# A two-layer mixer and experts kernel: three-part float32r products replaced by plain float32 products, experts' weights loaded in runs of 8 KB into 18 buffers

## The chip, the cores and the metric

The kernel runs on one core of one Trainium2 chip. The metric is the device time of one execution in microseconds (us); lower is better. Six units matter here: TensorE (PE in the profile, with its weight loads as PEld), VectorE (DVE), ScalarE (ACT), GpSimd (POOL), the queue of SyncE (SP) that issues most transfers, and the DMA engines that carry them out.

## What is computed

One sequence of 1024 tokens with 1024 features passes through two layers in float32. Each layer adds a mixer and then a routed block of experts, both on a normed and modulated input:

```
for i in range(2):
    shift1, scale1, gate1, shift2, scale2, gate2 = split(silu(c) @ ada_w[i] + ada_b[i], 6)
    h = modulate(rmsnorm(x, norm_mix_w[i]), shift1, scale1)
    y = even_mixer(h, ...) if i == 0 else odd_mixer(h, ...)
    x = x + gate1 * y
    h = modulate(rmsnorm(x, norm_ffn_w[i]), shift2, scale2)
    x = x + gate2 * hierarchical_moe(h, ...)
return rmsnorm(x, final_norm_w)
```

The even mixer is a product with `w_in` (1024 x 2048), a state space part with a gated product, stick-breaking attention over eight heads, and a product with `w_out`. The odd mixer has the same frame with a recurrence (rwkv7) and a second state space part (mamba2). Each token goes to two of 32 experts. An expert computes `(silu(x w_gate) * (x w_up)) w_down` with 1024 x 512, 1024 x 512 and 512 x 1024 weights: 6.29 MB per expert and layer, each read once from DRAM or, for an expert with more than 128 tokens, once per further block.

## The kernel before

**Products.** TensorE multiplies a stationary tile of 128 x 128 with a moving one of up to 512 columns and adds over blocks of 128 features. The large products are made in float32r, in three parts. `split` (L136) makes of a tile `x` a high part (a copy on ScalarE that rounds to float32r, L138) and a low part (`x` less the high part, on VectorE, L139). `mm3` (L237, products at L240 to L242) adds high x high, high x low and low x high into the same sum. For the experts the local function `three` does the same (L815 to L817), and `halves` (L803) splits a weight tile of 128 x 2048 in two pieces per part into rings of four tiles.

```
138        self.nc.scalar.activation(hi, x, AF.Copy)
139        self.nc.vector.tensor_tensor(lo, x, hi.bitcast(FT), op=OP.subtract)
240        nc.tensor.matmul(p, a[0], b[0], start=first, stop=False)
241        nc.tensor.matmul(p, a[0], b[1], start=False, stop=False)
242        nc.tensor.matmul(p, a[1], b[0], start=False, stop=last)
```

**Where three-part products stand.** Layer 0: the projections (`proj_T` and `proj_v`, 256 products of 512 columns), the gated product of the state space part (`glu`, 64), and the output product of tiles 2 to 7 (`out_rows`, 96; tiles 0 and 1 are made by plain float32 products at L681, ahead of the splitting of the output weights). Layer 1: the projections of the first half of the tokens (`o_group` and `m_dt`, 216), those of the second half (216), and the output product of the last three tiles (48). The projections of the second half run as work in the background: `project` is a generator that yields what each step is taken to cost (0.64 us per product), and `poke` draws 1.2 us worth of steps after each step of the recurrence. All else on TensorE, the transposes (L106) among it, is plain float32 or bfloat16.

**Experts (`moe`).** One block of 128 rows after another: 33 blocks written out per layer and more behind branches that the routing decides (two such blocks ran in layer 0). For a block, POOL gathers the rows (L786), `turn` transposes them (eight transposes into two PSUM tiles), eight products per part make the gate and eight the up product, ScalarE and VectorE make `silu(g) * u` (L831, L832), four transposes turn it, eight products make the two halves of the result, VectorE scales them (L847), and POOL scatters the rows to DRAM (L848). That is 24 products, 72 parts, and 12 transposes per block. PSUM holds one gate, one up, one hidden, two transposed and three result tiles. The products of one block and those of the next lie interleaved; a scheduler puts every engine's instructions in order when the kernel is built.

**Weights on their way.** `ring` opens pools of tiles of 128 x 2048 floats (1 MB); `wtile` takes them in turn. `wload` (L74) issues the load on SP's queue, with feature `k * 128 + p` on partition `p`, so that the runs in DRAM are 2 KB (gate, up) or 4 KB (down). The experts have 10 such buffers: `a0`, `c0`, `b0` with two each and `d0` with four in layer 0, `a1`, `c1`, `b1`, `e1` in layer 1. SP's queue works in order: a load that waits for its buffer holds up all loads behind it.

**Output stage.** `out_norm` (layer 1) and the end of `even` (layer 0) split the four output weight tiles once into `o["wp"]`, make the output product tile by tile, add it to the rows of x (loaded by SP, L1857 in layer 0) and route the tile (`out_route`). The four weight buffers are free as soon as they are split.

## Time and profile before

| | |
|---|---|
| runs shown | 3290.62, 3296.51, 3298.77 us; median 3296.51 us |
| profiled execution, span from first to last instruction | 3303.1 us (its own time is not listed apart) |
| instructions | 42136 |
| PE busy | 2817.3 us, 85% of the span, 15141 matmul records |
| DVE, ACT, POOL busy | 71%, 47%, 28% |
| moved by DMA | 704.06 MB, mean 213 GB/s |

The profile gives for each engine the time in which it worked on an instruction. Matmuls overlap, so a record's duration is longer than the distance to the next one; where the rate matters, the distance of starts is to be read. The granted clock of TensorE is given per stretch as a share of 2.4 GHz; 0.5 is its lower level of 1.2 GHz, and values between are means over both. A line of the code can be that of a helper, so L106 stands for every transpose.

### The profile page before, as it was taken

Reading aid. Unit: us, or ns where it says so; the run is one execution under the profiler, and the core shown is the slowest. Engines: PE = TensorE matmul, PEld = TensorE weight load, DVE = VectorE, ACT = ScalarE, POOL = GpSimd, SP = SyncE. Lnnn points to the kernel's source line nnn. Section 1 sums busy time; section 2 is a strip of 40 time slices with the busy share of each in tenths; the row PEclk is TensorE's granted clock in tenths of the full one; section 3 lists DMA queues with packets and bytes.
Section 4 is the critical chain, followed back from the end, with each engine's and each line's share of the span. In section 5 each row is a group of like instructions: output and inputs, shape, how many; then the busy total and the mean of one; then the engine's idle time right before and its main releaser. Section 6 shows DMA issues by size and latency. Waiting matters only on the chain. (4 is left out here: it accounts for less than half of the span.)

```text
span 3303.1 us, 42136 instructions
## 1 busy us (share of the span) xinstructions
PE 2817.3 (85%) x15141; PEld 2220.7 (67%) x15141; DVE 2350.0 (71%) x3738; ACT 1566.8 (47%) x2280; POOL 912.7 (28%) x1177
## 2 busy tenths in 40 slices
PE   5986788988899998997479999998895999998981
PEld 4775556656677776776367777776785777776761
DVE  7456998557789987886644445645558789987884
ACT  4211456333567766764334323332232667766661
POOL 4342654234221111110300533344125122111111
PEclk9987889988899999998689878887996999999996
DMA  8756201334899998984844522253355799998967
GB/s 274 162 146 162 78 15 46 109 131 145 308 292 380 354 338 293 343 278 160 273 147 129 175 65 86 74 138 101 97 190 206 275 293 373 360 338 302 350 243 297
DMA packets 473363, 704.06 MB, mean 213 GB/s; under 512 B 119681, under 2 KB 261025, under 8 KB 470577
## 3 DMA queue, kind: packets, MB, share of 16 engines
q1 hardware_dynamic: 400928, 642.69, 58.1%
q0 software_dynamic: 19872, 33.60, 2.8%
q10 hardware_dynamic: 52336, 24.87, 2.7%
q8 instruction: 128, 2.10, 0.3%
q14 instruction: 99, 0.80, 0.1%
HBM read 651.69 MB, written 88.16 MB: 224 GB/s over the span
## 5 line engine op out<-in xcount | busy, mean ns | idle before, releaser
L139 DVE TENSOR_TENSOR wlo<-w,whi 128x1024 fp32r<-128x1024 f32 x816 | 956.9, 1217 | 182.2 <-ACT whi L138 180.4
L138 ACT ACTIVATE whi<-w 128x1024 fp32r<-128x1024 f32 x816 | 811.0, 1052 | 415.3 <-PE ps_g L817 244.9
L240 PE MATMUL ps_b<-hTh,wh 128*128 128x512 f32 x608 | 261.8, 432 | 37.8 <-ACT cc L1242 21.2
L848 POOL DMA_INDIRECT ye_d<-y,tab x64 | 132.4, 2069 | 479.5 <-DVE y L847 393.5
L786 POOL DMA_INDIRECT xg<-h_d,tok x64 | 107.0, 1671 | 559.9 <-PE ps_t L106 525.9
L241 PE MATMUL ps_b<-hTl,wh 128*128 128x512 f32 x608 | 257.8, 424 | 0.3 <-DVE hTl L139 0.3
L242 PE MATMUL ps_b<-hTh,wl 128*128 128x512 f32 x608 | 256.2, 421 | 0.0
L816 PE MATMUL ps_g<-wlo,xh 128*128 128x512 f32 x544 | 228.1, 419 | 30.8 <-DVE wlo L139 30.7
L815 PE MATMUL ps_y<-whi,hh 128*128 128x512 f32 x544 | 225.2, 414 | 24.4 <-DVE y L847 11.4
L815 PE MATMUL ps_g<-whi,xh 128*128 128x512 f32 x544 | 224.8, 413 | 20.7 <-ACT xh L138 19.6
L817 PE MATMUL ps_g<-whi,xl 128*128 128x512 f32 x544 | 222.4, 409 | 1.6 <-DVE xl L139 1.4
L816 PE MATMUL ps_y<-wlo,hh 128*128 128x512 f32 x544 | 221.1, 406 | 0.0
L815 PE MATMUL ps_u<-whi,xh 128*128 128x512 f32 x544 | 217.1, 399 | 1.0 <-ACT whi L138 1.0
L816 PE MATMUL ps_u<-wlo,xh 128*128 128x512 f32 x544 | 216.3, 398 | 0.0
L817 PE MATMUL ps_u<-whi,xl 128*128 128x512 f32 x544 | 214.9, 395 | 0.0
L817 PE MATMUL ps_y<-whi,hl 128*128 128x512 f32 x544 | 212.0, 402 | 0.9 <-DVE hl L139 0.9
L139 DVE TENSOR_TENSOR wl<-w,wh 128x1024 fp32r<-128x1024 f32 x84 | 105.5, 1268 | 100.0 <-ACT wh L138 99.2
L240 PEld LDWEIGHTS ps_b<-hTh,wh 128*128 128x128 f32 x608 | 126.1, 208 | 67.4 <-ACT cc L1242 22.8
L167 DVE SCALAR_TENSOR_TENSOR adacc<-w,cs,adacc 128x256 f32<-128x256 f32 x329 | 163.5, 514 | 5.2
L138 ACT ACTIVATE wh<-w 128x1024 fp32r<-128x1024 f32 x84 | 86.3, 1053 | 161.2 <-PE ps_b L241 149.3
L816 PEld LDWEIGHTS ps_g<-wlo,xh 128*128 128x128 f32 x544 | 106.4, 196 | 68.1 <-DVE wlo L139 47.4
L313 DVE TENSOR_TENSOR_SCAN sP<-keep,sP,sbz 128x256 f32<-128x256 f32 (+1 forms) x160 | 131.5, 865 | 23.6 <-POOL keep L307 12.5
(658 smaller groups left out, 6039.9 us busy)
## 6 DMA issues: line engine op xcount, KB each, us to landing
w<-in_moe_w_down_dram SPq DMA_DIRECT2D x138, 1024.0 KB
w<-in_moe_w_up_dram SPq DMA_DIRECT2D x138, 1024.0 KB
w<-in_moe_w_gate_dram SPq DMA_DIRECT2D x138, 1024.0 KB
w<-in_ada_w_dram SPq DMA_DIRECT2D x48, 1024.0 KB
w<-in_odd_w_in_dram SPq DMA_DIRECT2D x26, 1024.0 KB
cy<-ye_d SPq DMA_DIRECT2D x16, 1024.0 KB
cx<-xm_d SPq DMA_DIRECT2D x29, 512.0 KB
w<-in_even_w_in_dram SPq DMA_DIRECT2D x8, 1024.0 KB
```

The lines of the kernel that those rows point to most:

```text
L138: self.nc.scalar.activation(hi, x, AF.Copy)
L139: self.nc.vector.tensor_tensor(lo, x, hi.bitcast(FT), op=OP.subtract)
L167: eng.scalar_tensor_tensor(acc, wk, ck, acc, op0=OP.mult, op1=OP.add)
L240: nc.tensor.matmul(p, a[0], b[0], start=first, stop=False)
L241: nc.tensor.matmul(p, a[0], b[1], start=False, stop=False)
L242: nc.tensor.matmul(p, a[1], b[0], start=False, stop=last)
L313: v.tensor_tensor_scan(P[:, r, 0:n][:, ::-1], keep[:, r, 0:n][:, ::-1], zero.to_broadcast([128, n]), P[:, r, n:n + 1], op0=OP.mult, op1=OP ...
L786: nc.gpsimd.indirect_dma_start(out=xg, out_offset=None, in_=h_d[:], in_offset=bass.IndirectOffsetOnAxis(ap=tokc, axis=0), bounds_check=T - ...
L815: nc.tensor.matmul(p, xh[:, k, :], w[0][:, j, ns], start=first, stop=False)
L816: nc.tensor.matmul(p, xh[:, k, :], w[1][:, j, ns], start=False, stop=False)
L817: nc.tensor.matmul(p, xl[:, k, :], w[0][:, j, ns], start=False, stop=last)
L848: nc.gpsimd.indirect_dma_start(out=ye_d[:], out_offset=bass.IndirectOffsetOnAxis(ap=asgc, axis=0), in_=y, in_offset=None, bounds_check=2 * ...
```

## The change

Every three-part product becomes one plain float32 product; `split`, `wsplit`, `mm3`, `halves` and `three` go, and with them all split tiles. Normed inputs are written once as float32; one saved half of the tokens in layer 1 goes to DRAM as one tensor of 2 MB instead of two. The experts' weights are loaded by `wload_runs` (L73 of the changed kernel): partition `p` takes the features `p * k` to `p * k + k - 1`, a run of 8 KB. So that the features meet, `turn` and the transposes of the hidden values read every fourth and every second column. The rings hold 18 buffers: `d0` has eight and a new ring `f0` four in layer 0, `e1` has 13 in layer 1. The generators of the background work yield 0.43 per product. The output weights are used from the buffers into which they were loaded.

```
+    def wload_runs(self, src, k):
+        w = self.wtile()
+        self.nc.sync.dma_start(w, src.rearrange("(p k) n -> p (k n)", k=k))
+        return w[:].rearrange("p (k n) -> p k n", k=k)
...
     def proj_T
-                self.mm3(p[:, h, :], [x[:, k, col:col + 128] for x in w], [x[:, k, ts] for x in hs], k == 0, k == KD - 1)
+                self.nc.tensor.matmul(p[:, h, :], w[:, k, col:col + 128], hT[:, k, ts], start=(k == 0), stop=(k == KD - 1))
...
     def turn
-                    self.transpose(pt[:, q * 128:(q + 1) * 128], xg[:, (hh * 4 + q) * 128:(hh * 4 + q + 1) * 128])
-                self.split(xh[:, 4 * hh:4 * hh + 4, :].rearrange("p k t -> p (k t)"),
-                           xl[:, 4 * hh:4 * hh + 4, :].rearrange("p k t -> p (k t)"), pt)
+                cols = xg[:, hh * 512:(hh + 1) * 512].rearrange("t (p k) -> t k p", k=4)
...
+                    self.transpose(pt[:, q * 128:(q + 1) * 128], cols[:, q, :])
+                if hh == 0:
+                    nc.scalar.activation(o, pt, AF.Copy)
+                else:
+                    nc.vector.tensor_copy(o, pt)
...
     def expert
-                for h in range(2):
-                    w = halves(ww[h])
-                    for k in range(4):
-                        three(p, x, 4 * h + k, w, k, slice(0, 512), h == 0 and k == 0, h == 1 and k == 3)
+                for k in range(KD):
+                    nc.tensor.matmul(p, x[:, k, :], ww[k // 4][:, k % 4, :], start=(k == 0), stop=(k == KD - 1))
...
+                cols = hs[:, (q // 2) * 256:(q // 2) * 256 + 256].rearrange("t (p k) -> t k p", k=2)
+                self.transpose(pt[:, q * 128:(q + 1) * 128], cols[:, q % 2, :])
...
-            for f2 in range(2):
-                w = halves(ws[2][f2])
-                for f in range(2):
-                    for n in range(2):
-                        three(py[n], h, 2 * f2 + f, w, f, slice(n * 512, (n + 1) * 512), f2 == 0 and f == 0, f2 == 1 and f == 1)
+            for f in range(4):
+                for n in range(2):
+                    nc.tensor.matmul(py[n], h[:, f, :], ws[2][f // 2][:, f % 2, n * 512:(n + 1) * 512],
+                                     start=(f == 0), stop=(f == 3))
...
     def o_group
-            self.mm3(p, [x[:, k, :] for x in w], [x[:, k, :] for x in hs], k == 0, k == KD - 1)
-            yield 0.64
+            self.nc.tensor.matmul(p, w[:, k, :], hs[:, k, :], start=(k == 0), stop=(k == KD - 1))
+            yield 0.43
...
     def even
-            o["wp"] = [self.wsplit(w, wx, 4) for w in o["ws"]]
...
-            keep.enter_context(self.ring("d0", 4))
+            keep.enter_context(self.ring("d0", 8))
             right.close()
+            keep.enter_context(self.ring("f0", 4))
...
-        c1.enter_context(k.ring("e1", 5))
+        c1.enter_context(k.ring("e1", 13))
```

The order of instructions moves at two places. First TensorE in the expert loop of layer 0, once it is even. `ps_g` and `ps_u` are the gate and up sums, `ps_y` the result, `ps_t` transposed rows, `ps_h` transposed hidden values; `whi`, `wlo`, `xh`, `xl` are high and low parts. Before, a piece of one block:

```order
L106 MATMUL ps_h<-ident,hs 128x128 x4
L106 MATMUL ps_t<-ident,xg_6610 128x128 x8
L815 MATMUL ps_u<-whi,xh 128x512
L816 MATMUL ps_g<-wlo,xh 128x512
L817 MATMUL ps_g<-whi,xl 128x512
```

In the changed kernel, one whole block:

```order
L111 MATMUL ps_t<-ident,xg_5571 128x128 x4
L784 MATMUL ps_g<-w,xt 128x512 x4
L111 MATMUL ps_t<-ident,xg_5573 128x128 x4
L111 MATMUL ps_h<-ident,hs 128x128 x4
L784 MATMUL ps_u<-w,xt 128x512 x3
L784 MATMUL ps_g<-w,xt 128x512 x4
L784 MATMUL ps_u<-w,xt 128x512 x3
L798 MATMUL ps_y<-w,hh 128x512 x8
L784 MATMUL ps_u<-w,xt 128x512 x2
```

A block's 72 parts are 24 products, still interleaved with those of the next block, and the result's eight stand together; products of another block stand between the hidden transposes and the result that needs them.

Second, SP's queue from the output stage of layer 0 on. `xo` are the rows of x that the output product is added to. Before:

```order
L1857 DMA xo<-in_x_dram 128x1024 x2
L77 DMA w<-in_moe_w_down_dram 128x2x1024 x2
L77 DMA w<-in_moe_w_up_dram 128x4x512 x2
L77 DMA w<-in_moe_w_gate_dram 128x4x512 x2
L1857 DMA xo<-in_x_dram 128x1024 x6
L77 DMA w<-in_moe_w_gate_dram 128x4x512 x2
```

In the changed kernel:

```order
L1807 DMA xo<-in_x_dram 128x1024 x2
L76 DMA w<-in_moe_w_down_dram 128x2048 x2
L76 DMA w<-in_moe_w_gate_dram 128x2048 x2
L76 DMA w<-in_moe_w_up_dram 128x2048 x2
L76 DMA w<-in_moe_w_down_dram 128x2048 x2
L76 DMA w<-in_moe_w_gate_dram 128x2048 x2
L1807 DMA xo<-in_x_dram 128x1024 x5
L76 DMA w<-in_moe_w_up_dram 128x2048 x2
L76 DMA w<-in_moe_w_gate_dram 128x2048 x2
L1807 DMA xo<-in_x_dram 128x1024
```

More of the experts' weights are asked for ahead of the rows, and the last load of rows, that of tile 7, has moved behind the up and gate loads of the first expert (the four just ahead of it), which take the buffers `c0` and `a0` that hold the output weights.

## Rows read from the trace of the kernel before

**Rows 1.** The page, first lines: the span, and busy time per engine.

```profile
span 3303.1 us, 42136 instructions
PE 2817.3 (85%) x15141; PEld 2220.7 (67%) x15141; DVE 2350.0 (71%) x3738; ACT 1566.8 (47%) x2280; POOL 912.7 (28%) x1177
```

**Rows 2.** The page's groups: count, busy us, mean ns, idle time before.

```profile
L139 DVE TENSOR_TENSOR wlo<-w,whi 128x1024 fp32r<-128x1024 f32 x816 | 956.9, 1217 | 182.2 <-ACT whi L138 180.4
```

**Rows 3.** Timeline of PE in the expert loop: start, us, instruction, idle before.

```profile
1059.74 0.50 PE L816 MATMUL ps_g<-wlo,xh 128*128 128x512 f32 x1 [0.45 <-DVE wlo L139]
1060.07 0.39 PE L817 MATMUL ps_g<-whi,xl 128*128 128x512 f32 x1
...
1062.40 0.39 PE L815 MATMUL ps_g<-whi,xh 128*128 128x512 f32 x1
1062.63 0.60 PE L106 MATMUL ps_h<-ident,hs 128*128 128x128 f32 x4
...
1063.86 0.48 PE L815 MATMUL ps_u<-whi,xh 128*128 128x512 f32 x1
...
1078.55 0.50 PE L816 MATMUL ps_g<-wlo,xh 128*128 128x512 f32 x1 [0.45 <-DVE wlo L139]
```

**Rows 4.** Timeline of weight loads at the plain products of layer 0.

```profile
701.95 0.19 PEld L681 LDWEIGHTS ps_e<-w,gl 128*128 128x128 f32 x1 [0.24 <-issue]
...
707.10 0.19 PEld L681 LDWEIGHTS ps_e<-w,qT 128*128 128x128 f32 x1 [0.24 <-issue]
```

**Rows 5.** Instructions on tile `ps_e`: count, duration min/median/max ns, first and last start.

```profile
L681 PE MATMUL ps_e<-w,gl x32: 592/592/697, 648.3 to 704.5; 128*128 128x512 f32 x32
```

**Rows 6.** Timeline of DVE: first and 33rd block of layer 0, then layer 1.

```profile
853.29 0.68 DVE L832 TENSOR_TENSOR hs<-hs,ps_u 128x512 f32<-128x512 f32 x1
...
1505.79 0.68 DVE L832 TENSOR_TENSOR hs<-hs,ps_u 128x512 f32<-128x512 f32 x1
...
2576.33 0.68 DVE L832 TENSOR_TENSOR hs<-hs,ps_u 128x512 f32<-128x512 f32 x1
...
3229.39 0.69 DVE L832 TENSOR_TENSOR hs<-hs,ps_u 128x512 f32<-128x512 f32 x1 [0.42 <-PE ps_u L817]
```

**Rows 7.** Stretches: us, busy (instructions) per engine, granted clock, DMA share, GB/s.

```profile
1021.00:1136.00 115.00, 112.16 (x516) 89.91 (x516) 106.46 (x111) 85.34 (x100) 22.97 (x14) 1.00 1.01 360
1250.00:1345.00 95.00, 82.24 (x354) 64.62 (x355) 76.24 (x80) 60.44 (x70) 12.57 (x9) 0.96 0.87 300
...
3260.00:3280.00 20.00, 0.00 (x0) 0.00 (x0) 15.09 (x15) 3.45 (x6) 4.49 (x3) 0.50 1.02 425
```

**Rows 8.** Stretches, line L240 alone (first parts): us, PE, PEld, clock, DMA.

```profile
59.00:290.00 231.00, 106.67 (x256) 51.52 (x256) 0.93 0.64 166
555.00:648.00 93.00, 27.09 (x64) 12.54 (x64) 0.93 0.27 80
708.00:799.00 91.00, 38.85 (x96) 18.00 (x96) 1.00 0.43 145
1600.00:1840.00 240.00, 93.72 (x224) 44.09 (x224) 0.87 0.55 184
1840.00:2200.00 360.00, 92.84 (x208) 43.97 (x208) 0.85 0.32 89
2453.00:2506.00 53.00, 20.05 (x48) 9.33 (x48) 0.96 0.56 204
```

**Rows 9.** The background stretch of layer 1, all instructions, columns as in rows 7.

```profile
1840.00:2200.00 360.00, 353.99 (x2640) 273.69 (x2639) 192.35 (x373) 113.52 (x223) 152.13 (x388) 0.85 0.32 89
```

**Rows 10.** Waits of PE in 59 to 290 us: total us, times, longest.

```profile
PE ps_e L179 <- DVE adacc L167: 10.9, 5, 3.4
PE ps_b L240 <- ACT hTh L138: 8.7, 1, 8.7
```

**Rows 11.** Timeline at the start of layer 0's experts: SP's queue, then PE.

```profile
709.98 76.30 SPq L1857 DMA_DIRECT2D xo<-in_x_dram  x6
...
797.79 0.39 PE L242 MATMUL ps_e<-wh,yl 128*128 128x512 f32 x1
...
838.35 1.94 PE L106 MATMUL ps_t<-ident,xg 128*128 128x128 f32 x8 [21.07 <-issue]
```

More of the change, by code (lines that the diff above doesn't have):

```diff
@@ L10 @@
 FT = mybir.dt.float32
-FR = mybir.dt.float32r
 BF = mybir.dt.bfloat16
@@ L755, in out_norm @@
                 else:
-                    yt = self.out_y(o, t, y_d)
-                    y = [oy.tile([128, KD, 128], FR, name=n) for n in ("yh", "yl")]
-                    self.split(*y, yt)
-                    x = self.out_rows(o, t, lambda k: [h[:, k, :] for h in y], "a")
+                    y = self.out_y(o, t, y_d)
+                    x = self.out_rows(o, t, lambda k: y[:, k, :], "a")
                 self.out_route(o, t, x, "bcb")
@@ L1173, in odd_setup @@
         R["cc"] = one.tile([128, 8, 3], FT, name="cc")
-        R["wd"] = [one.tile([128, KD, 8], FR, name=n) for n in ("wdh", "wdl")]
-        self.split(*R["wd"], R["wdt"])
         R["tk"] = one.tile([128, NT, 2, 8], FT, name="tk")
@@ L1211, in m_dt @@
         for k in range(KD):
[L1212 to L1213 removed]
+            nc.tensor.matmul(p[0:8, :], R["wdt"][:, k, :], hs[:, k, :], start=(k == 0), stop=(k == KD - 1))
+            yield 0.43
         nc.scalar.activation(xx, p[0:8, :], AF.Identity, bias=R["dtb"])
@@ L1698, in odd @@
             pj = right.enter_context(tc.tile_pool(name="wsp1", bufs=1, side="right"))
-            hs = [hp.tile([128, KD, 512], FR, name=n) for n in ("hTh", "hTl")]
+            hs = hp.tile([128, KD, 512], FT, name="hT")
             rw = [(128 * c, self.rw_shift, c) for c in (12, 4, 6, 0, 2, 8, 10)]
@@ L1715, in getx @@
                     return x, junk, junk
-                ht = [np_.tile([128, KD, 512], FR, name=n) for n in ("tTh", "tTl")]
+                ht = np_.tile([128, KD, 512], FT, name="tT")
                 for t in range(4):
@@ L1736, in project @@
                     for z in range(2):
-                        w = [pj.tile([128, KD, 128], FR, name=x, bufs=2) for x in ("wh", "wl")]
-                        self.split(*w, src[:, :, 128 * z:128 * z + 128])
-                        yield from do(h, c + z, w, hs, R, pj)
+                        yield from do(h, c + z, src[:, :, 128 * z:128 * z + 128], hs, R, pj)
                     pos[0] = n + 1
@@ L1938, in out @@
                 ts = slice(t * 128, (t + 1) * 128)
-                if t < XA:
-                    return self.out_rows(o, t, lambda k: gl[:, k, ts] if k < 4 else qT[:, k - 4, ts], "e")
-                y = [wx.tile([128, KD, 128], FR, name=n) for n in ("yh", "yl")]
-                for z, src in enumerate((gl, qT)):
-                    self.split(*(x[:, 4 * z:4 * z + 4] for x in y), src[:, :, ts])
-                return self.out_rows(o, t, lambda k: [x[:, k, :] for x in y], "e")
+                return self.out_rows(o, t, lambda k: gl[:, k, ts] if k < 4 else qT[:, k - 4, ts], "e")
             def route(t, x):
@@ L1974, in even @@
             keep.enter_context(self.ring("b0", 2))
-            parts = ExitStack()
-            wx = pool(parts, "wx0", "left")
-            o["wp"] = [self.wsplit(w, wx, 4) for w in o["ws"]]
             for t in range(NT):
```

108 lines of the change are left out of this document (32 added, 76 removed).

## The prediction

> **What bounds the kernel now.** I read the busy shares first: TensorE is busy for 2817 of 3303 us, VectorE for 71% [rows 1]. Shares are averages, so I went to the expert loops, where 33 blocks per layer stand between 853.29 and 1505.79 us and between 2576.33 and 3229.39 us [rows 6]: 32 intervals in 652.5 and 653.1 us, 20.4 us a block. The reader should see that this is not one limit but two that alternate. At its tightest a block takes 18.81 us, and TensorE idles once in it, 0.45 us, for a low part of the weights [rows 3]; over 1021 to 1136 us it is busy 112 of 115 us at full clock. From 1250 to 1345 us four blocks take some 23.5 us each, TensorE is busy 82 of 95 us, and the DMA moves only 300 GB/s at a share of 0.87 [rows 7]: weights come late there, because a load must wait until a buffer has been split. So the loop is TensorE's at best (18.8) and the weights' at worst, 20.4 in the mean.
>
> Outside the loops the three-part products stand in six stretches; their counts of first parts, and so of products, are 256, 64, 96, 224, 208 and 48, together 896 (layer 1's projections are cut at 1840 us) [rows 8]. In the long background stretch of layer 1 TensorE is busy 354 of 360 us at a granted clock of 0.85 of full speed (a mix of 1.2 and 2.4 GHz) [rows 9].
>
> **The price of one product.** Eleven parts start from 1060.07 to 1062.40 us, ten steps of 0.233 us; that makes 0.699 us for a three-part product of 512 columns [rows 3]. The kernel before already holds plain float32 products of the same shape: the first two output tiles of layer 0. They have 32 records for 2 tiles x 2 halves x 4 feature blocks = 16 products [rows 5], two records each. Thirteen weight loads of such records start from 701.95 to 707.10 us, in twelve even steps: 0.429 us a record, **0.858 us a plain product** [rows 4]. The change therefore costs 0.159 us per product wherever TensorE sets the pace. That is the number the forecast rests on; the instruction count falls to a third, the time does not.
>
> **Part 1, the expert blocks.** 24 products: 24 x 0.858 = 20.6 us. Twelve transposes take 1.23 us (1062.63 to 1063.86) [rows 3]. Of the tight block 18.81 - 72 x 0.233 - 1.23 = 0.80 us is left for joints; 0.45 of that is the wait for a split, which goes, 0.4 stays. Sum 22.2. The transposes now read every fourth (rows) or every second (hidden) float, because the weights lie in runs of 8 KB and the features must be dealt out the same way. No row shows such a read; I bound it by nothing below and by twice the transposes' 0.103 us each above, 0 to 1.2 us a block, and take 0.1, near the rows that exist. **22.3 us a block.** The splits (VectorE 957 us over both loops [rows 2], ScalarE nearly as much) were beside TensorE's work, so removing them returns only the 1.6 us by which the mean block exceeds the tight one; that cover is gone as the limit moves to TensorE. Against 20.4: +1.9 x 66 = **+125 us**.
>
> Does the DMA keep up? A block needs 6.29 MB of weights and some 0.5 MB of rows, 6.8 MB in 22.3 us = 305 GB/s. The loop reached 360 GB/s over 1021 to 1136 us; a stretch that reads runs of 8 KB (the expert outputs, at the end) and writes reaches 425 [rows 7]. With 18 buffers, 12 blocks' parts ahead of the 6 in use, a slow stretch is bridged. So the long runs and the buffers are worth nothing beyond the 1.6 us already counted. A buffer is now held until the product has read it, not only until it was split; that is what the eight more buffers pay for.
>
> The Trainium skill, "SBUF — State Buffer" (The DMA port swizzle), speaks against part of this: SBUF has lines of 16 bytes, and a reader needs two hits a line for full speed, which every fourth float does not give. No run here shows it; by that page the row transposes would be slower, and by rival 2 below the sum would be 47 us more.
>
> **Part 2, the start of the loops.** In layer 0 the four buffers that the first expert's gate and up weights take still hold the output weights, which formerly were split away. The order shows these four loads now ahead of the last load of x rows on SP's queue; they wait for the last output product, and the row load behind them waits too. Before, the last x load had been issued 76.30 us after 709.98, so 11.5 us ahead of the last output part at 797.79, and 40.6 us passed from there to the first expert transposes at 838.35 [rows 11]. Four loads of 1.05 MB at 300 to 360 GB/s [rows 7] are 12 to 14 us. Routing of the tile before hides about half: +7 us, ends 0 and +13. In layer 1 two of these loads stood there before: +4, same ends. **+11 us.**
>
> **Part 3, the other products.** At 0.159 us each: 40.7, 10.2, 15.3, 35.6, 33.1 and 7.6, together 142 us. What absorbs some:
> - Layer 0's projections wait 10.9 us for partial sums of the conditioning and 8.7 for a split of the normed rows [rows 10]. A later TensorE hides most of the first, and the modulation without its split shortens the second; VectorE is relieved in the norm as well: -22, leaves +18.
> - The gated product of layer 0: a little split waiting goes, +6. Output tiles: +15, nothing covers them.
> - Layer 1, first half of the tokens: the norm loses two passes per quarter tile on ScalarE and VectorE: -10, +25.
> - The background stretch has 6 us of idle time in 360 [rows 9], so nearly all stays: +28. Its generators count a step as 0.43 instead of 0.64, so three products go between two foreground steps where two went; the same work stands earlier, in total no less. The output tiles after it: +7.
>
> **+99 us**; ends 60 (twice the cover) and 142 (none). VectorE's removed splits in these stages are else beside TensorE, so nothing more comes back.
>
> **Sum.** 125 + 11 + 99 = +235 us on the span of 3303.1, so 3538 us. The page gives this execution's span and no further time of its own; the span is 6.6 us above the median of the runs, 3296.5. Moving the median by the same 235 gives **3531 us**.
>
> **Rivals.**
> 1. **A plain product costs one record, not two.** If its two records overlapped, or a product took one, it would cost 0.43 us, the figure that the pacing of the background work uses. A block would fall to 24 x 0.43 + 1.6 = 11.9 us and the weights would set 6.8 MB / 360 GB/s = 18.8: -1.6 x 66 = -106; the others 896 x 0.27 = -241, of which some 190 count: about 3000 us. It decides at about 0.75 us per product, where 235 us over some 2,280 effective products is gone. Against it stand the counts [rows 5] and the even spacing [rows 4]. Chance 0.03; some idle time of TensorE (486 us in all) shrinking more than I count could bring no change or a small gain, 0.03 more.
> 2. **The strided transposes.** If the eight row transposes take twice their 0.103 us, a block takes 0.8 us instead of 0.1 more: +0.7 x 66 = +47, 3578 us. For it: it is an access no row covers, and all of it is on TensorE's path. The page named in part 1 says that such a read is slow. Against: the weight load of a transpose runs beside the one before. Chance 0.14.
> 3. **The DMA becomes the limit.** If the runs of 8 KB move at 250 GB/s, a block takes 27 us: +4.9 x 66 = 323 more, some 3850 us. For it: the loop was short of weights at 300 GB/s in one stretch. Against: 425 GB/s at a share of 1.02 elsewhere [rows 7]. Chance 0.06.
>
> That the splits might stay in the program is excluded by the order: no such row is left on VectorE.
>
> **Numbers.** The forecast has 0.74, rivals 0.26. Low end: a block at 21.8 (-33), twice the cover in part 3 (-39), no late start (-11): 3448, rounded to 3440. High end: rival 2 (+47), no cover (+43), late starts in full (+15): 3636, rounded to 3640. Beyond lie rivals 1 and 3, together about 0.1, and the sizes I misjudge. A measurement of this kernel tells 0.3%, 10 us, from no change. Faster 0.04 (rival 1 and part of the idle time), same 0.02, slower 0.94.
>
> **What would show it.** In the profile after: two records per product, 0.43 us apart; blocks spaced 22 to 23 us by the product of the hidden values, evenly, without the 24 to 26 us ones; TensorE above 95% in the loops at full clock; VectorE and ScalarE far below; DMA about 300 GB/s and below its full share. Transposes further apart than 0.103 us would mean rival 2, TensorE idle before products and a full DMA share rival 3. A last x load issued only after the last output product would confirm part 2. I am wrong if products start closer than 0.8 us, or if the blocks are not TensorE's.

## The result and the profile after

The changed kernel takes 3513.1 us (median of 4 runs, 3506.1 to 3522.5), the kernel before 3295.0 us (4 runs): a ratio of 1.066, 95% interval 1.064 to 1.069, 218 us slower. The forecast was 3531 us, slower, range 3440 to 3640.

The first lines of the page of the changed kernel answer to [rows 1]. TensorE's share rises from 85 to 90% with fewer records; VectorE's falls from 71 to 35%, ScalarE's from 47 to 18%.

```profile
span 3520.8 us, 34468 instructions
PE 3176.6 (90%) x12613; PEld 1748.9 (50%) x12613; DVE 1225.1 (35%) x2643; ACT 625.4 (18%) x1251; POOL 758.8 (22%) x1177
```

TensorE's timeline in layer 0's expert loop, one block (start, us, instruction), is the counterpart of [rows 3]. There is no idle time in it, and every product shows as two records.

```profile
1094.80 0.63 PE L111 MATMUL ps_t<-ident,xg 128*128 128x128 f32 x4
1095.27 3.60 PE L784 MATMUL ps_g<-w,xt 128*128 128x512 f32 x8
1098.71 0.63 PE L111 MATMUL ps_t<-ident,xg 128*128 128x128 f32 x4
1099.18 0.65 PE L111 MATMUL ps_h<-ident,hs 128*128 128x128 f32 x4
1099.66 2.74 PE L784 MATMUL ps_u<-w,xt 128*128 128x512 f32 x6
1102.24 3.60 PE L784 MATMUL ps_g<-w,xt 128*128 128x512 f32 x8
1105.67 2.74 PE L784 MATMUL ps_u<-w,xt 128*128 128x512 f32 x6
1108.25 7.03 PE L798 MATMUL ps_y<-w,hh 128*128 128x512 f32 x16
1115.11 1.88 PE L784 MATMUL ps_u<-w,xt 128*128 128x512 f32 x4
1116.83 0.63 PE L111 MATMUL ps_t<-ident,xg 128*128 128x128 f32 x4
```

Sixteen records of the result start from 1108.25 to 1115.11 us: 6.86 / 16 = 0.429 us each, 0.858 us a product, the price that the forecast took from [rows 4]. The whole block, from 1094.80 to 1116.83, takes 22.03 us = 24 x 0.858 + 1.44 for the twelve transposes. VectorE's timeline at the product of the hidden values, first and last of the 33 blocks per layer with one step of the even part, answers to [rows 6]:

```profile
890.92 0.69 DVE L788 TENSOR_TENSOR hs<-hs,ps_u 128x512 f32<-128x512 f32 x1 [14.52 <-PE ps_t L111]
...
1117.09 0.69 DVE L788 TENSOR_TENSOR hs<-hs,ps_u 128x512 f32<-128x512 f32 x1 [1.08 <-PE ps_u L784]
1139.11 0.69 DVE L788 TENSOR_TENSOR hs<-hs,ps_u 128x512 f32<-128x512 f32 x1 [1.08 <-PE ps_u L784]
...
1601.20 0.69 DVE L788 TENSOR_TENSOR hs<-hs,ps_u 128x512 f32<-128x512 f32 x1 [1.09 <-PE ps_u L784]
2734.13 0.69 DVE L788 TENSOR_TENSOR hs<-hs,ps_u 128x512 f32<-128x512 f32 x1 [13.86 <-PE ps_u L784]
...
3448.60 0.69 DVE L788 TENSOR_TENSOR hs<-hs,ps_u 128x512 f32<-128x512 f32 x1 [1.09 <-PE ps_u L784]
```

That is 22.20 and 22.33 us a block in the mean, against 20.39 and 20.41. In each layer 24 of the 32 intervals are even, 22.01 to 22.03 us; the first seven are longer, up to 24.0 us in layer 0 and 27.7 in layer 1, so the forecast's "without the 24 to 26 us ones" held for all but the start of the loop. Stretches of the two loops (us, busy per engine, granted clock, DMA share, GB/s) answer to [rows 7]: TensorE busy without a gap at full clock, the DMA at four fifths of its share.

```profile
1100.00:1580.00 480.00, 480.00 (x1305) 229.78 (x1304) 57.82 (x87) 36.58 (x66) 43.57 (x43) 1.00 0.79 289
2950.00:3420.00 470.00, 470.00 (x1279) 225.07 (x1278) 56.09 (x84) 36.06 (x64) 42.56 (x42) 1.00 0.82 301
```

**Where the time went.** Each stage below runs from one instruction's start to another's, read from the timelines: the last output product and the first product of hidden values ("loop start"), the 33rd of these, the first projection product of layer 1, the first and the last output product of its last tiles. The last two columns belong to the two half changes of the first experiments.

| stage (us) | forecast | before | after | difference | outside alone | experts alone |
|---|---|---|---|---|---|---|
| start to layer 0's last output product | +39 | 797.8 | 833.1 | +35.3 | +30.2 | -10.9 |
| to layer 0's loop start | +7 | 55.5 | 57.8 | +2.3 | +8.9 | -6.0 |
| 32 intervals of blocks | +61 | 652.5 | 710.3 | +57.8 | +2.7 | +57.8 |
| to layer 1's first projection product | in the next | 107.6 | 93.0 | -14.6 | -6.2 | -10.2 |
| layer 1's mixer | +53 | 840.1 | 912.3 | +72.2 | +76.1 | -10.0 |
| its last output products | +7 | 51.8 | 64.9 | +13.1 | +14.6 | +0.9 |
| to layer 1's loop start | +4 | 70.9 | 62.7 | -8.2 | +1.4 | -10.2 |
| 32 intervals of blocks | +61 | 653.1 | 714.5 | +61.4 | +10.0 | +61.8 |
| to the end | 0 | 73.7 | 72.2 | -1.5 | -1.1 | +0.2 |

Stages outside the loops come from one profile each. Kernels here that share the code outside the experts differ by up to 14 us in the first stage (783.5 to 797.8) and 28 in layer 1's mixer (830.1 to 858.2), so a single difference there is not known to better than that. Means over the six kernels of this document with three-part products outside the experts, and over the six with plain products there and no product left out, are steadier: 788.3 and 830.4 us in the first stage, 843.7 and 907.8 in the mixer, +42 and +64. The block rows repeat within 0.4 us in every kernel that shares the changed loop and its runs of 8 KB.

### The profile page after: what moved, and what is told of

It is laid out like the page before. It is cut to its first block, busy times and chain, and to the rows that moved or that the text cites. A ratio compares the mean times of both kernels' runs of the same rounds, so it can differ in the third digit from the quotient of the medians.

```text
span 3520.8 us, 34468 instructions
## 1 busy us (share of the span) xinstructions
PE 3176.6 (90%) x12613; PEld 1748.9 (50%) x12613; DVE 1225.1 (35%) x2643; ACT 625.4 (18%) x1251; POOL 758.8 (22%) x1177
## 5 line engine op out<-in xcount | busy, mean ns | idle before, releaser
L784 PE MATMUL ps_u<-w,xt 128*128 128x512 f32 x1088 | 497.4, 592 | 0.0
L784 PE MATMUL ps_g<-w,xt 128*128 128x512 f32 x1088 | 495.3, 595 | 1.3 <-ACT xt L772 1.2
L798 PE MATMUL ps_y<-w,hh 128*128 128x512 f32 x1088 | 482.5, 596 | 3.0 <-ACT hh L794 2.2
L803 DVE TENSOR_TENSOR y<-ps_y,g2row 128x512 f32<-128x512 f32 x136 | 94.0, 692 | 1107.1 <-PE ps_y L798 1107.1
L1138 PE MATMUL ps_b<-hT,w 128*128 128x512 f32 x832 | 388.7, 623 | 10.5 <-ACT cc L1196 10.5
L798 PEld LDWEIGHTS ps_y<-w,hh 128*128 128x128 f32 x1088 | 207.0, 191 | 260.9 <-issue 256.7
L784 PEld LDWEIGHTS ps_u<-w,xt 128*128 128x128 f32 x1088 | 203.3, 191 | 235.8 <-issue 235.3
L784 PEld LDWEIGHTS ps_g<-w,xt 128*128 128x128 f32 x1088 | 201.5, 192 | 223.1 <-issue 220.2
L1138 PEld LDWEIGHTS ps_b<-hT,w 128*128 128x128 f32 x832 | 162.3, 200 | 200.6 <-issue 186.4
L772 ACT ACTIVATE xt<-ps_t 128x512 f32<-128x512 f32 x68 | 40.6, 597 | 826.6 <-PE ps_t L111 826.6
L233 PE MATMUL ps_b<-hT,w 128*128 128x512 f32 x384 | 175.9, 617 | 5.6 <-ACT hT L222 2.9
L295 DVE TENSOR_TENSOR_SCAN sP<-keep,sP,sbz 128x256 f32<-128x256 f32 (+1 forms) x160 | 135.3, 885 | 39.9 <-POOL keep L289 25.7
L787 ACT ACTIVATE hs<-ps_g 128x512 f32<-128x512 f32 x68 | 40.6, 598 | 533.5 <-PE ps_g L784 533.5
L138 POOL TENSOR_TENSOR rs<-rm,nhalf 128x1 f32<-128x1 f32 (+2 forms) x56 | 51.8, 926 | 333.7 <-DVE rm L136 218.7
L233 PEld LDWEIGHTS ps_b<-hT,w 128*128 128x128 f32 x384 | 74.6, 197 | 96.2 <-issue 88.7
L297 POOL TENSOR_TENSOR sw<-sw,sP 128x512 f32<-128x512 f32 (+1 forms) x80 | 93.2, 1167 | 134.5 <-ACT sw L284 66.5
```

What stands on the lines that cost most here:

```text
L138: nc.gpsimd.tensor_tensor(r, m, self.nhalf[:, 0:n], op=OP.pow)
L233: self.nc.tensor.matmul(p[:, h, :], w[:, k, col:col + 128], hT[:, k, ts], start=(k == 0), stop=(k == KD - 1))
L295: v.tensor_tensor_scan(P[:, r, 0:n][:, ::-1], keep[:, r, 0:n][:, ::-1], zero.to_broadcast([128, n]), P[:, r, n:n + 1], op0=OP.mult, op1=OP ...
L297: g.tensor_tensor(w[:, :, 0:n], w[:, :, 0:n], P[:, :, 1:n + 1], op=OP.mult)
L784: nc.tensor.matmul(p, x[:, k, :], ww[k // 4][:, k % 4, :], start=(k == 0), stop=(k == KD - 1))
L798: nc.tensor.matmul(py[n], h[:, f, :], ws[2][f // 2][:, f % 2, n * 512:(n + 1) * 512], start=(f == 0), stop=(f == 3))
```

## The experiments

**The two halves of the change.** Outside alone: the expert loops of the kernel before in the changed kernel. Experts alone: the changed `moe` and rings in the kernel before.

The core of the first, against the changed kernel (the rings go back to 10 buffers with it):

```
-                for k in range(KD):
-                    nc.tensor.matmul(p, x[:, k, :], ww[k // 4][:, k % 4, :], start=(k == 0), stop=(k == KD - 1))
+                for h in range(2):
+                    w = halves(ww[h])
+                    for k in range(4):
+                        three(p, x, 4 * h + k, w, k, slice(0, 512), h == 0 and k == 0, h == 1 and k == 3)
...
-            return [[self.wload_runs(a[n][i, e, h * m:(h + 1) * m], k) for h in range(2)] for n, k, m in names]
+            return [[self.wload(a[n][i, e, h * m:(h + 1) * m], k) for h in range(2)] for n, k, m in names]
```

The core of the second, against the kernel before (the loading changes with it, as in the change):

```
-                for h in range(2):
-                    w = halves(ww[h])
-                    for k in range(4):
-                        three(p, x, 4 * h + k, w, k, slice(0, 512), h == 0 and k == 0, h == 1 and k == 3)
+                for k in range(KD):
+                    nc.tensor.matmul(p, x[:, k, :], ww[k // 4][:, k % 4, :], start=(k == 0), stop=(k == KD - 1))
...
+            keep.enter_context(self.ring("f0", 8))
...
-        c1.enter_context(k.ring("e1", 5))
+        c1.enter_context(k.ring("e1", 13))
```

> Half of the change alone: plain products, without splits, outside the experts; the expert loops as before (three-part products, runs of 2 and 4 KB, 10 buffers). By the stages of the two traces the expert blocks cost 57.8 + 61.4 us in the change; without them and without the 8.4 us that the blocks behind the branches gave back, some 106 us remain. Theory (the two halves add up): 3395 to 3410 us, expert blocks of 20.4 us in the mean. Rival A (the faster ends of the output stages come from the relieved loops, so the halves do not add up): 3410 to 3425 us. Rival B (the uncovered price of the products outside was overestimated from the stages, the loops' start shifts it): below 3380 us.

> The other half of the change: expert loops as in the changed kernel (plain products, runs of 8 KB, 18 buffers), three-part products with their splits everywhere else. Plain products outside alone gave 3438 us, 140 more than before; the whole change gives 3513. Theory A (the halves only add; what is missing, 75 us, is what the experts cost): 3370 to 3378 us. Theory B (the blocks cost 119 us wherever they stand, less 8 us in the blocks behind the branches, and the loops start 8 to 10 us earlier per layer when the first expert needs no splits beside the routing): 3385 to 3395 us. Theory C (the loops cost 119 us, and no start gets faster): 3405 us or more. Blocks of 22.0 us in all three.

Outside alone: 3438.4 us against 3297.8 (ratio 1.043, interval 1.039 to 1.047), +141. Experts alone: 3380.3 against 3293.5 (1.026, 1.024 to 1.029), +87. Together 227, against 218 for the whole. I had expected at most 3425 us for the first, so the stage sums had misled me: every bound I wrote was passed. The table shows where: the loops' starts gain 6.0 and 10.2 us from the experts' half and lose 8.9 and 1.4 from the other, which the whole change shows only as about their sum, +2.3 and -8.2; and the old loops, with code that is unchanged, came out 2.7 and 10.0 us longer. The second lies between theories A and B, with blocks of 22.20 and 22.34 us, as in the whole change: the blocks cost 119 us. By the medians 32 us of it are given back; the table shows 16.2 at the loops' starts, and the two blocks behind the branches take 47.8 us instead of 56.3.

One of these gains can be seen on POOL, whose timeline shows the first gather of rows. First the kernel before, VectorE and then POOL; then the changed kernel; then experts alone:

```profile
821.28 9.16 DVE L139 TENSOR_TENSOR wlo<-w,whi 128x1024 fp32r<-128x1024 f32 x8
```

```profile
821.94 9.67 POOL L786 DMA_INDIRECT xg<-h_d,tok  x1 [6.98 <-ACT whi L138]
```

```profile
864.82 1.29 POOL L757 DMA_INDIRECT xg<-h_d,tok  x1 [6.94 <-DVE q_w L913]
```

```profile
809.91 1.29 POOL L790 DMA_INDIRECT xg<-h_d,tok  x1 [6.98 <-DVE q_w L946]
```

The gather that the first expert waits for took 9.67 us while VectorE made the first expert's eight low parts, and 1.29 us without them; in layer 1 it is 9.63 and 1.17 us. Three later runs, described below, have three-part products everywhere outside the experts and keep the split experts (one of them in five weight tiles of six), but their first gather is short in one layer, and these starts are as early as without splits. In layer 0 the loop starts 54.2 to 56.4 us after the last output product in the four such kernels whose gather took 9.7 us, 46.6 us in the one whose gather took 1.91 us (ten half tiles), and 49.5 us with experts alone. In layer 1 it takes from the first output product to the loop's start 122.8 to 124.4 us in the three kernels with a gather of 9.6 us or more, 111.6 and 112.5 us in the two with one of 1.2 us (half tiles, one whole tile), and 113.4 us with experts alone. So the gain goes with the gather, not with the splits as such. In the run with ten half tiles VectorE made its low parts beside the short gather of layer 0 and the two behind it (VectorE, then POOL):

```profile
806.12 11.44 DVE L139 TENSOR_TENSOR wlo<-w,whi 128x1024 fp32r<-128x1024 f32 x10 [0.42 <-ACT whi L138]
```

```profile
806.60 1.91 POOL L786 DMA_INDIRECT xg<-h_d,tok  x1 [4.05 <-DVE tok L1021]
808.81 1.68 POOL L786 DMA_INDIRECT xg<-h_d,tok  x1 [0.30 <-issue]
810.79 1.96 POOL L786 DMA_INDIRECT xg<-h_d,tok  x1 [0.30 <-issue]
```

**Run length.** The changed kernel with the old loading:

```
-            return [[self.wload_runs(a[n][i, e, h * m:(h + 1) * m], k) for h in range(2)] for n, k, m in names]
+            return [[self.wload(a[n][i, e, h * m:(h + 1) * m], k) for h in range(2)] for n, k, m in names]
...
-                cols = xg[:, hh * 512:(hh + 1) * 512].rearrange("t (p k) -> t k p", k=4)
+                cols = xg[:, hh * 512:(hh + 1) * 512].rearrange("t (k p) -> t k p", k=4)
```

> The changed kernel, but the experts' weights are loaded as before, in runs of 2 KB and 4 KB, and the transposes read neighbouring columns again; 18 buffers stay. Theory (a block is TensorE's: 24 products of 0.858 us and 12 transposes, 22.03 us in the trace of the changed kernel): only the strided transposes can give something back. The 12 transposes took 22.03 - 20.59 = 1.44 us against 1.23 us in the kernel before, so a block falls to 21.8 us and the total by 0.2 x 66 = 14 us, to about 3500 us; the share of the DMA engines rises from 0.8 towards 0.87 and hides it. Rival A (the runs of 8 KB are what lets the weights keep up): blocks of 23 to 24 us as in the slow stretch of the kernel before, TensorE idle before products, 3570 us or more. Rival B (strided reads cost much): the transposes take less than half their time, blocks of 21.3 us, 3465 us.

3502.4 us, ratio 1.063 (1.060 to 1.067), 11 us below the changed kernel, as the theory has it. The even blocks are 21.91 us, the mean is 0.11 us shorter in layer 0 and 0.17 in layer 1, so the strided transposes cost 0.11 us a block. Their weight loads show the read itself, below the contiguous one of this run, then the two strided ones of the changed kernel, rows at every fourth float and hidden values at every second (min/median/max in ns):

```profile
L111 PEld LDWEIGHTS ps_t<-ident,xg x544: 138/141/231, 871.8 to 3411.8; 128*128 128x128 f32 x182
```

```profile
L111 PEld LDWEIGHTS ps_t<-ident,xg x544: 195/208/261, 873.7 to 3427.0; 128*128 128x128 f32 x182
L111 PEld LDWEIGHTS ps_h<-ident,hs x272: 194/211/221, 892.1 to 3449.7; 128*128 128x128 f32 x136
```

A load gets 0.07 us longer (that of the hidden values from 0.140 to 0.211), but most of it runs beside the matmul ahead of it: the transposes start 0.12 us apart instead of 0.11. The long runs are a small loss here.

**Ten buffers.** The changed kernel with as many buffers as before:

```
-            keep.enter_context(self.ring("d0", 8))
+            keep.enter_context(self.ring("d0", 4))
-            keep.enter_context(self.ring("f0", 4))
-        c1.enter_context(k.ring("e1", 13))
+        c1.enter_context(k.ring("e1", 5))
```

> The changed kernel with 10 weight buffers in each expert loop, as before the change, instead of 18; runs of 8 KB stay. Theory (TensorE sets the block): a load lands some 6 us after its issue (median 5.2 to 6.9 us in the changed kernel), four buffers ahead of the six in use are 4 x 3.67 = 14.7 us of work, so blocks stay at 22.03 us and the total within 10 us of 3513. Rival (the eight buffers pay for being held until the product has read them): TensorE idles before products for the DMA, blocks of 23 us or more, 3580 us or more.

3505.8 us (1.064, 1.061 to 1.067); blocks of 22.03 us, TensorE busy without a gap in this stretch too. The eight buffers buy nothing in the loop.

```profile
1100.00:1580.00 480.00, 480.00 (x1307) 229.93 (x1306) 58.75 (x88) 36.67 (x65) 43.58 (x43) 1.00 0.81 298
```

**What the loading could do.** Half of the products left out, with long and with short runs:

```
-                for k in range(KD):
+                for k in range(0, KD, 2):
...
-            for f in range(4):
+            for f in range(0, 4, 2):
```

> The changed kernel with every second product of the expert blocks left out (12 of 24; all weights are still loaded, and a buffer is held until its last remaining product); the output is not the reference's. TensorE then needs 12 x 0.858 + 1.44 = 11.7 us a block, so that the weights must set the pace: this measures what the loading in runs of 8 KB can do. Theory: 366 GB/s at full share, as in the loops of the changed kernel, 6.8 MB in 18.6 us a block, some 3295 us in all. Rival A: the runs of 8 KB reach the 425 GB/s of the last stage, 16.0 us a block, 3130 us. Rival B (my third rival: 250 GB/s): 27 us a block, slower than the changed kernel.

> The same half of the products left out (the output is not the reference's), with the weights loaded as before, in runs of 2 KB and 4 KB, and contiguous transposes; 18 buffers. Beside the run with runs of 8 KB it shows what the long runs are worth where TensorE is not the limit. Theory: the short runs cost 3 to 5% of the DMA's time (share 0.83 to 0.86 for 288 to 304 GB/s, against 0.79 to 0.82 for 289 to 301): 19.2 us a block, some 3330 us. Rival: no difference, the same blocks within 0.2 us. Rival B: the short runs cost 10% or more, 20.5 us a block, 3410 us.

One run each: 3136 and 3200 us. The first 32 intervals of layer 0 take 503.95 and 536.4 us, 15.75 and 16.76 us a block; in layer 1 16.81 and 17.72. My ceiling of 366 GB/s, scaled up from a share of 0.8, was wrong; the blocks are near those of rival A, at 389 GB/s in the mean of the stretch below; single blocks take 8 to 38 us, so only the mean can be read. Stretches of the two, long runs first:

```profile
982.00:1380.00 398.00, 300.09 (x838) 147.22 (x837) 59.25 (x94) 41.09 (x69) 46.17 (x46) 0.89 0.96 389
```

```profile
998.00:1419.00 421.00, 301.57 (x837) 142.13 (x837) 59.29 (x94) 41.09 (x69) 46.28 (x46) 0.87 1.00 371
```

Long runs move 5% more and save 1.0 us a block, but only where TensorE needs 11.7 us. Either loading, with 18 buffers, feeds a block in under 18 us; the DMA is far from bounding the changed kernel.

**Long runs in the kernel before.** Three-part products and 10 buffers, only the loading and the transposes of the change:

```
-            return [[self.wload(a[n][i, e, h * m:(h + 1) * m], k) for h in range(2)] for n, k, m in names]
+            return [[self.wload_runs(a[n][i, e, h * m:(h + 1) * m], k) for h in range(2)] for n, k, m in names]
...
-                    self.transpose(pt[:, q * 128:(q + 1) * 128], xg[:, (hh * 4 + q) * 128:(hh * 4 + q + 1) * 128])
+                    self.transpose(pt[:, q * 128:(q + 1) * 128], cols[:, q, :])
```

> The kernel before with nothing changed but the loading: runs of 8 KB and strided transposes; three-part float32r products and 10 buffers stay. Theory (the loss is the products alone, the loading is a small gain where the weights set the pace): the changed kernel moves 289 to 301 GB/s at a DMA share of 0.79 to 0.82, some 366 GB/s at full share, where the kernel before moves 322 at 0.92, some 350; the 1.6 us by which its mean block exceeds its tightest falls by half at most, less 0.2 us for the transposes: blocks of 19.8 to 20.4 us, 3250 to 3300 us. Rival (the short runs are what starves the loop before): blocks of 19.0 us throughout, 3205 us. Rival B (strided reads are what makes the changed kernel slower): blocks above 21 us, 3340 us or more.

3298.1 us, ratio 1.001 (0.999 to 1.002): nothing. The slow stretch keeps its blocks, 25.9, 24.4, 20.8 and 23.3 us against 25.7, 24.7, 20.8 and 23.4 in the kernel before, whose layer 1 has the same slow ones at the same place (26.3, 24.6, 20.8 and 23.3):

```profile
1250.00:1345.00 95.00, 86.34 (x382) 69.54 (x381) 78.11 (x81) 60.94 (x71) 14.34 (x9) 0.98 0.85 310
```

So what I had read from [rows 7], "weights come late there", is false. The waits of ScalarE in 1250 to 1345 us of the kernel before (us in total, times, longest) say what comes late: the split tiles, which products have not yet read. SP's queue does wait for buffers to be split, 86.5 of the 95 us (last line), but no engine waits for a load in this stretch.

```profile
ACT whi L138 <- PE ps_g L817: 16.3, 8, 3.6
ACT whi L138 <- PE ps_y L817: 13.1, 4, 5.6
SPq L77 <- DVE wlo L139: 86.5, 27, 7.0
```

**Split tiles in the kernel before.** Three attempts on that wait: half-size tiles; ten of these instead of eight, with 8 load buffers; and one weight tile of six left whole.

```
-        hl = ctx.enter_context(tc.tile_pool(name=f"hl{i}", bufs=4))
+        hl = ctx.enter_context(tc.tile_pool(name=f"hl{i}", bufs=8))
...
-            hi, lo = (hl.tile([128, 2048], FR, name=n) for n in ("whi", "wlo"))
+                hi, lo = (hl.tile([128, 1024], FR, name=n) for n in ("whi", "wlo"))
```

> The kernel before with one edit: the split tiles of the experts' weights are 8 half tiles of 128 x 1024 per part instead of 4 whole ones, the same memory, each with its own release. Theory (in its slow blocks ScalarE waits for products to give a split tile free, 33 of 95 us from 1250 to 1345 us, and the loads wait for the splits; the weights themselves could come in 16 to 18 us a block, as with half the products): split tiles come free earlier, blocks fall from 20.4 towards the tightest, 18.8 to 19.6 us, total 3200 to 3250 us. Rival (the order in which the blocks were laid out makes the slow blocks, not the number or size of the split tiles): blocks of 20.2 to 20.5 us, total within 10 us of 3297.

The second has this beside it:

```
+        hl = ctx.enter_context(tc.tile_pool(name=f"hl{i}", bufs=10))
...
-            keep.enter_context(self.ring("d0", 4))
+            keep.enter_context(self.ring("d0", 2))
...
-        c1.enter_context(k.ring("e1", 5))
+        c1.enter_context(k.ring("e1", 3))
```

> The kernel before with 10 half split tiles per part (a quarter more split memory) and 8 load buffers instead of 10. Theory (the ring of split tiles is what binds): at least as fast as 8 half tiles, blocks of 18.8 to 19.4 us, 3190 to 3240 us. Rival A (order): within 10 us of 3297. Rival B (with 8 buffers, two ahead of the six in use, the weights come late: 2 x 3.1 us of work ahead against some 6 us from issue to landing): blocks of 21 us or more, above 3320 us.

3293.0 us (0.999, 0.998 to 1.001) and 3309.0 us (1.005, 1.003 to 1.006). The first has blocks from 17.0 to 28.3 us in another pattern and the same mean, 20.45 and 20.12; the second has even blocks of 20.49 us in 26 of 32 intervals, with a mean of 20.81 and 20.80. The size of the split tiles does not set the mean. Their number was raised only together with a cut of the load buffers, so what more split tiles alone would give is not shown.

The third:

```
+            hf = sb.tile([128, 2, 128], FT, name="hf")
+            nc.scalar.activation(hf[:].rearrange("p k t -> p (k t)"), pt[:, 256:512], AF.Copy)
...
+                    nc.tensor.matmul(py[n], hf[:, f, :], ws[2][1][:, f, n * 512:(n + 1) * 512], start=False, stop=(f == 1))
```

> The kernel before with one weight tile of six per expert block left whole: the four products of the second down tile are plain, on a plain copy of the hidden values; the other 20 products stay three-part. VectorE's own work per block falls from some 17.7 us (12 low parts of 1.217 us, five steps of 0.68 us) by 2 x 1.217 + 0.3 us to 15.0, the splits on ScalarE by 2 us, TensorE's grows by 4 x 0.159 = 0.64 us to 18.6 with the transposes. Theory (the blocks of 20.4 us come from VectorE and TensorE, both close to 18 us a block, waiting for each other through the split tiles; neither the DMA nor the split tiles' number alone mattered): blocks of 19.0 to 19.7 us, total 3210 to 3255 us, faster than both kernels. Rival A (TensorE and the order set the block): blocks of 20.9 to 21.1 us, 3330 to 3345 us. Rival B (it cancels): 20.4 us, within 10 us of 3295.

3439.9 us (1.044, 1.042 to 1.047), blocks of 22.87 and 22.72 us, worse than each of the three expectations, though VectorE is busy for only 67% of the loop's time. The new order makes TensorE wait for the rows' high part in almost every block, 31 times in layer 0's loop (timeline of TensorE, then stretches with the granted clock):

```profile
1215.20 1.04 PE L106 MATMUL ps_t<-ident,xg 128*128 128x128 f32 x8
1216.95 0.66 PE L106 MATMUL ps_h<-ident,hs 128*128 128x128 f32 x4 [0.72 <-DVE hs L832]
1219.17 0.71 PE L815 MATMUL ps_g<-whi,xh 128*128 128x512 f32 x1 [1.56 <-ACT xh L138]
1219.68 0.63 PE L816 MATMUL ps_g<-wlo,xh 128*128 128x512 f32 x1
```

```profile
1208.00:1215.00 7.00, 7.00 (x28) 4.86 (x27) 4.55 (x5) 3.48 (x5) 1.01 (x1) 1.00 0.71 260
1219.10:1222.30 3.20, 3.13 (x8) 2.45 (x9) 3.20 (x5) 0.78 (x3) 0.00 (x0) 0.53 1.02 345
```

Two waits of 0.72 and 1.56 us around the transposes, and then seven steps of parts 0.43 us apart instead of 0.233, at a granted clock of 0.53, near the lower level: 7 x 0.2 = 1.4 us, as if the longer wait were paid nearly twice. This run lightened VectorE and changed the order at once, so it does not tell what a lighter VectorE in the old order would give. ScalarE stands behind VectorE's low part of the hidden values before its new copy `hf` in each block. I found no version that beats both kernels.

**Pace of the background work.**

```
-            yield 0.43
+            yield 0.86
```

> The changed kernel with the background generators yielding 0.86 per product, what a product takes, instead of 0.43. Theory (layer 1's mixer cost what its products cost, 72 us more where 432 products x 0.159 = 69 us): where the products stand does not matter, the total stays within 10 us of 3513, and the end of the last background product only moves later. Rival (the background is used up too early): after it ends, TensorE runs at a granted clock of 0.71 for 364 us in the changed kernel, against 0.85 for 258 us in the kernel before; spread out, it gives 20 to 50 us back, 3465 to 3495 us.

3514.0 us (1.067, 1.064 to 1.070), no change. Layer 1's mixer is 12.2 us shorter in its profile (900.1 us), and 2.0 and 6.7 us are lost again in the output products and before the loop starts. The last stretch of the recurrence runs at a granted clock of 0.77 instead of 0.71; the first row is the changed kernel's, the second this one's, the third that of the run with ten buffers:

```profile
2240.00:2604.00 364.00, 318.71 (x2520) 268.48 (x2519) 164.91 (x331) 97.54 (x255) 125.99 (x285) 0.71 0.38 104
```

```profile
2240.00:2600.00 360.00, 318.59 (x2559) 264.20 (x2558) 169.06 (x332) 97.41 (x256) 128.57 (x285) 0.77 0.41 106
```

```profile
2240.00:2604.00 364.00, 327.23 (x2554) 269.61 (x2553) 177.98 (x335) 97.67 (x258) 123.63 (x264) 0.77 0.39 108
```

The run with ten buffers has the changed kernel's pace, and its mixer takes 900.8 us at the same granted clock, so neither is shown to come from the pace.

**The late x rows.** Tile 7's rows get a tile of their own and are loaded first:

```
+                    x = pool.tile([128, D], FT, name="xo7", bufs=1)
+                    with self.tc.high_priority(offset=1000):
+                        nc.sync.dma_start(x, x_src[t * 128:(t + 1) * 128, :])
```

> The changed kernel, with the x rows of tile 7 in layer 0 in a tile of their own, loaded ahead of all other loads of the output stage, so that they no longer stand behind the first expert's loads. Theory: from the start of the last output product to the first expert transposes it takes 40.6 us in the kernel before and in the changed one alike, so the late load is on no path: total within 8 us of 3513, the first transposes within 3 us of 873.7 us. Rival (my part 2: the late load costs some 7 us; VectorE waits 10 us for x rows in the changed kernel): first transposes 7 to 13 us earlier, total 3500 to 3506 us.

3514.8 us (1.065, 1.062 to 1.069), no change. SP's queue now issues that load at 658.91 us instead of 834.22 (the first line is the changed kernel's), and the first expert transposes start 39.3 us after the last output product (831.9 us) instead of 40.6:

```profile
834.22 0.33 SPq L1807 DMA_DIRECT2D xo<-in_x_dram  x1
```

```profile
658.91 0.34 SPq L1812 DMA_DIRECT2D xo<-in_x_dram  x1
```

```profile
871.22 1.10 PE L111 MATMUL ps_t<-ident,xg 128*128 128x128 f32 x4 [13.53 <-issue]
```

## Why the prediction was right, and where it was not

**The price: right.** 0.858 us a product, as read from [rows 4]. It held in the loops and outside, and rival 1 was out.

**Part 1: right in size, partly for the wrong reason.** Forecast +1.9 us a block, measured +1.81 and +1.92 (57.8 and 61.4 us over 32). The terms of an even block: products 20.59 as forecast, transposes and strided reads 1.44 where I had 1.23 + 0.1, joints none where I had kept 0.4. Strided reads cost 0.11 us; I had taken 0.1. Rival 2 was right that the read is slower, a load grows from 0.14 to 0.21 us, and wrong in the price: the loads run beside other work. By the Trainium skill, "SBUF — State Buffer" (Door 1: The DMA port swizzle), an access that does not hit a 16-byte line twice is slowed. The loads at every fourth float, 208 ns against 141, agree; those at every second float hit each line twice and took 211 against 140 all the same, which that rule does not explain. The block hardly notices either.

What was wrong is why the old mean of 20.4 us stood 1.6 above its tight blocks of 18.8. I said late weights. No engine waits for a load in the slow stretch, runs of 8 KB do not change it, and with half of the products the blocks are fed in 16 to 18 us. The number came out because I took the mean from [rows 6] and the new block from TensorE alone, so that the wrong reason entered no term. The mean is not explained: half tiles, and ten of them with fewer load buffers, leave it at 20.1 to 20.8 us, and the one run with less work on VectorE, in another order, made it worse. VectorE and ScalarE wait for TensorE there and TensorE for them, in an order laid out when the kernel is built. The same blocks are slow in both layers, which fits such an order; that it is the cause was argued, not tried.

**Rival 3: out, by more than I thought.** The DMA moves 389 GB/s over 398 us when asked to; 301 were needed. That the long runs and buffers are worth nothing beyond was right: undoing either gives 11 and 7 us less, not more, about what the intervals can tell.

**Part 2: wrong.** I forecast +11 us for the starts, from the x load behind the first expert's loads. The order was as described, the last load was issued only at 834.22 us, after the start of the last output product (833.1), the sign that I had named for part 2; but it costs nothing: taken away, nothing happens. The starts gave -5.9 us in all, as a loss of 10.3 with the plain products outside and a gain of 16.2 with the unsplit experts. For the gain the gather is the mechanism that the rows show. Of the loss I can say only that in layer 0 the first gather starts 31.7 us after the last output product instead of 24.2.

Loads do cost something at the start of layer 0, but others than I named. In the changed kernel four more loads of experts' weights are issued from 860.33 us, and while the first gather waits for its rows the DMA is at its full share; with ten buffers it is not (stretches from the first gather's start to the first expert transposes, the changed kernel first):

```profile
864.80:873.70 8.90, 0.00 (x0) 0.01 (x1) 0.00 (x0) 0.00 (x0) 3.28 (x3) 0.50 1.00 407
```

```profile
863.50:868.30 4.80, 0.04 (x1) 0.07 (x1) 0.59 (x2) 0.00 (x0) 3.28 (x3) 0.50 0.46 128
```

With ten buffers the loop starts 50.8 us after the last output product instead of 57.8; some 4 of these 7 us are the gather's.

**Part 3: right in sum, cover misjudged in place.** Forecast +99, measured +35.3 - 14.6 + 72.2 + 13.1 = +106, of which 8.5 us were given back in the two blocks behind the branches (56.3 to 47.8 us), which I had not counted here. Layer 0 was forecast +39 and gave +35 (42 between the means over six kernels). In layer 1's mixer little or nothing covered the products: 432 x 0.159 = 69 us, measured 72, between the means 64. Some 6 us came back ahead of its first product; that it is the relieved norm that returned them is not shown. The pace of the background products did not matter for the time.

**The sum.** +235 forecast, +218 measured: 17 us too much in part 2, 6 in part 1, 7 too little in part 3, and 1.5 at the end that I had not counted. That the misses go both ways and partly cancel is luck.

## What to carry to other kernels

Price a change of number format by the distance of starts of the very instruction, if the kernel holds one already, and not by the count of instructions: a third of the parts took 23% longer here (0.858 against 0.699 us). Ask of each engine that gets relieved whether anything waited for it; VectorE and ScalarE lost about half of their work or more and that gave back only some 30 us. Before a slow stretch is put down to late transfers, look whether any engine waits for a load there, and halve the work to see how fast the transfers can come.

## What the hardware showed that I had not expected

- A gather issued by POOL took 9.67 us instead of 1.29 while VectorE made eight low parts of the kind SBUF minus SBUF, 9.16 us in all; it ended 1.2 us after them. In layer 1 it took 9.63 and 1.17 us. With ten low parts in a row (ten half tiles, layer 1) it took 11.90 us and ended 1.1 us after them. By the Trainium skill, "SBUF — State Buffer" (SBUF: two separate sides), VectorE with two SBUF inputs and a GpSimd operation that reads SBUF exclude each other for one instruction. These rows agree that the one waits for the other, but here POOL did not get in between eight or ten instructions. Layer 0 of the run with ten half tiles speaks against making a rule of it: three gathers of 1.7 to 2.0 us passed while ten low parts stood back to back. Why POOL waited for the whole row in one case and not in the other stays open.
- In the run with one whole weight tile, twelve transposes with waits of 0.72 and 1.56 us behind them were followed by parts 0.43 us apart at a granted clock of 0.53, until 1222.67 us, and then by 0.233 us again. A short wait in a loop at full clock cost more there than its own length.
- The DMA moved 389 GB/s over 398 us with runs of 8 KB and 371 with runs of 2 and 4 KB, both at nearly full share. Throughput at a share of 0.8, scaled up to one (366), had put the ceiling too low.
